# A decoder block on one core: bias copies issued one at a time, one conditional block in place of two, and 28 low parts on GpSimd

## The chip, the cores and the metric

The kernel runs on one core of a Trainium2 chip. The metric is the device time of one execution in microseconds (us). Engines are named as in the profile: PE (TensorE), PEld (its weight loads), DVE (VectorE), ACT (ScalarE), POOL (GpSimd) and SP (SyncE, which here only issues transfers).

## The reference

One layer of a decoder block on 512 tokens of width 1024, in float32. A wide input projection feeds two branches:

```
proj = jnp.einsum('bsd,de->bse', x, w_in[l])
(q_a, k_a, v_a, iq, ik, iw, q_r, k_r, v_r, g_r, gate_a, gate_r) = jnp.split(proj, offsets, axis=-1)
...
_, sel = lax.top_k(score, k_sel)                       # 128 keys of each query, by an indexer's score
bias = rel_bias[t5_bucket(posb[:, :, None] - pos_g)]   # by distance of positions, for 8 heads
logits = einsum(q, k_g) * dh**-0.5 + bias              # softmax over the chosen keys
...
h = sigmoid(gate_a) * (y_a @ w_attn_branch) + sigmoid(gate_r) * (y_r @ w_ret_branch)
x = layer_norm(ALPHA * x + h @ w_out);  x = layer_norm(ALPHA * x + relu(x @ w_up)**2 @ w_down)
```

`y_a` is the sparse attention, `y_r` a chunkwise retention (512 tokens in four chunks, rotated queries and keys). The positions given are 0 to 511, so each step from one token to the next is 1; the kernel must also be right for others.

## The kernel before

**Units.** All weights come in 140 units: units 0 to 7 are 128x324 (index projection), all others 128x1024, which is two blocks of 128 rows by 512 columns. Units 8 to 11 make `ka`, 12 to 15 `qa`, 16 to 19 `va`, 20 to 23 `qr`, 24 to 27 `kr`, 28 to 35 `vr`, 36 to 43 `gr`; then come the gates and branches, the output projection and the MLP. SP loads a unit (`load_unit`, tile `raw`, 4 buffers), ACT makes its high part (`split_hi`, `whi`, 3 buffers), DVE its low part `raw - whi` (`split_lo`, `wlo`, 3 buffers), and PE multiplies three times for each product (`mm3`): high by high, low by high, high by low. A unit of two blocks is thus 24 matmuls of 512 columns, for four banks (`group`). When the last unit of a group is done, an engine reads its four PSUM banks out (tag `m`, 4 buffers), so the first matmul of the next group waits until a bank has been read. For `qr` and `kr` that is DVE (`rope_evac`: one product into tile `rt` and two half products, L670 and L673), and POOL adds the two (`rnat`).

**What runs between.** At each step of a group a `tick` moves queued tasks on: the rotation tables, the index scores and their top 128 (`topk_task`: 16 rounds of MAX and MATCH_REPLACE on DVE for each of three query blocks; the mask `mk` of a block is the last of it), and the attention. An attention task needs a tile `bm`: a piece of the bias, loaded by SP from a DRAM tensor `bd` (`bm_task`), to which POOL adds the mask. So `bm` loads stand on SP's queue between the loads of units, and POOL's additions come in the order of its queue.

**The bias.** `bias_by_distance` makes one row `R8` of biases by distance for each head. For even positions eight transfers from ACT's queue (`bias_even`, 7.15 MB in all) lay that row out in DRAM as `bd`, once for each query. `uneven` is 0 when every step of the positions is 1. The function `bias` is called twice, behind the group of `ka` for heads 0 to 3 and behind that of `qa` for heads 4 to 7: each call loads `uneven` into a register of every engine and opens a conditional block, in which the four transfers stand. The second call has an other branch, `bias_general`, which makes the bias for any positions, with matmuls on PE; it is not run here. Its instructions stand in each engine's program all the same, and an engine skips them with an unconditional branch.

**What sets the order.** The program is recorded in the order of the code, and a scheduler then orders each engine's instructions inside a block by a simulated timeline; no instruction crosses the border of a conditional block. On the chip each engine runs its list in order.

Of the kernel before, what the change touches and what calls it, by code (L numbers as in the profile page):

```python
# [11 lines left out]
F32 = mybir.dt.float32  # L12
# [47 lines left out]
class Build:  # L60
# [67 lines left out]
    def split_hi(self, i):  # L128
        if i >= len(self.units) or i in self.whi:
            return  # L130
        hi = self.w.tile([P, *self.units[i][1:]], F32R, tag="whi", name=f"whi{i}", bufs=3)
        self.nc.scalar.copy(hi, self.raw[i])  # L132
        self.whi[i] = hi

    def split_lo(self, i):
# [3 lines left out]
        self.nc.vector.tensor_sub(lo, self.raw.pop(i), self.whi[i].bitcast(F32))  # L139
# [118 lines left out]
    def setup_small(self):  # L258
# [3 lines left out]
        self.posq = sm.tile([P, 4], I32, name="posq")  # L262
        nc.sync.dma_start(self.posq, d["posq"])
# [25 lines left out]
    def bias_tables(self):  # L289
# [9 lines left out]
        self.rbd = sm.tile([P, 3, 4, H], BF16, name="rbd")  # L299
        nc.vector.memset(self.rbd, 0.0)  # L300
        for q in range(4):
            r = slice(32 * q, 32 * q + 32)
            nc.vector.tensor_copy(self.rbd[r, :, q, :], parts[r])
# [36 lines left out]
    def bias_general(self):  # L340
        run, todo = [], [self.bias_prep()] + [self.bias_task(j, G) for j in range(NS) for G in range(8)]
        while run or todo:
            if todo:
                run.append(todo.pop(0))
            for g in list(run):
                if next(g, self) is self:
                    run.remove(g)

    def bias_by_distance(self):
# [5 lines left out]
        for i, sl in enumerate((slice(0, S), slice(S, W))):  # L355
# [4 lines left out]
            for p in range(3):  # L360
                nc.tensor.matmul(ps[:H, :n], lhsT=self.rbd[:, p, 0, :], rhs=oh[i][:, :n],
                                 start=p == 0, stop=p == 2)
# [3 lines left out]

    def bias_even(self, hs):

        for j in range(NS):
            w = self.pitch(j) + 1  # L370
            row = self.R8[hs, S - P * (j + 1):S - P * (j + 1) + w]
            src = bass.AP(tensor=row.tensor, offset=row.offset, ap=[[0, P], row.ap[0], row.ap[1]])
            self.nc.scalar.dma_start(self.bd[j][hs, :P * w].rearrange("h (q w) -> q h w", q=P), src)

    def bias_prep(self):

        nc = self.nc
        self.nd = []
        for j in range(NS):
            K = P * (j + 1)  # L380
            dn = self.alloc(dt=I32, name="dn")
            nc.gpsimd.tensor_tensor(dn[:, :K], self.posq[:, j:j + 1].to_broadcast([P, K]),
                                    self.posk[:, :K], op=OP.subtract)
            nv = self.allocs(2, name="nv")
            n, v = nv[0][:, :K], nv[1][:, :K]
            nc.vector.tensor_scalar(n, dn[:, :K], 0.0, NMAX, op0=OP.max, op1=OP.min)
            nc.vector.tensor_scalar(v, n, 1.0, None, op0=OP.max)
            nc.scalar.activation(v, v, AF.Ln, scale=0.0625)
            nc.vector.tensor_scalar(v, v, 16 / math.log(8), -0.49, op0=OP.mult, op1=OP.add)
            nc.vector.tensor_scalar(v, v, MAGIC, MAGIC - 1, op0=OP.add, op1=OP.max)  # L390
            nc.vector.tensor_scalar(v, v, MAGIC - 1, None, op0=OP.subtract)
            nb = self.alloc(dt=BF16, name="nb")
            nc.vector.scalar_tensor_tensor(nb[:, :K], n, 15.0, v, op0=OP.min, op1=OP.add)
            nd = self.dr.tile([P, K], BF16, name=f"nd{j}")
            nc.sync.dma_start(nd, nb[:, :K])
            self.free(dn, nb, nv)
            self.nd.append(nd)
            yield

    def bias_task(self, j, G):  # L400

        nc = self.nc
        K, C = P * (j + 1), P * j + 16 * (G + 1)
        while len(self.nd) <= j:
            yield
        yield from self.need(4)
        st = self.allocs(2, shape=(P, 2, K), dt=BF16, name="bst")
        for i in range(2):
            src = self.nd[j][16 * G:16 * G + 16, :].rearrange("(q g) k -> q g k", q=4)
            src = src[:, 2 * i:2 * i + 2].rearrange("q g k -> q (g k)")  # L410
            nc.sync.dma_start(st[i].rearrange("p g k -> p (g k)"),
                              src[:, None, :].to_broadcast([4, 32, 2 * K]))
        yield
        yield
        oh = self.allocs(2, shape=(P, 2, C), dt=BF16, name="boh")
        for i in range(2):
            nc.vector.tensor_scalar(oh[i], st[i][:, :, :C], self.bucket, None, op0=OP.is_equal)
        self.free(st)
        yield
        ps = self.ps.tile([P, S], F32, tag="s", name="bps", bufs=3)  # L420
        for p in range(3):
            for g in range(4):
# [720 lines left out]
```

## Time and profile before

| | |
|---|---|
| median of three runs | 893.34 us (891.0 to 894.33) |
| the profiled execution | 893.39 us, of which the profile's span is 891.6 us |
| PE busy | 852.8 us (96%) |
| DVE, ACT, POOL busy | 497.5 (56%), 300.2 (34%), 119.4 us (13%) |
| mean granted TensorE clock | 0.985 of full |

The profiled execution is as long as the median of the runs. PE is busy nearly all the time, so the time of the kernel is that of PE's matmuls and of the places where PE stands. "Busy" adds up instructions; the waits of an engine are listed by what released them. The granted clock is 1.00 at 2.4 GHz and 0.50 at 1.2 GHz.

### The profile page before, as it was taken

How to read it: one execution, taken by the hardware profiler on the slowest of the kernel's cores; microseconds unless marked ns; L12 is line 12 of the kernel's file. 1: busy time of each engine (PE TensorE's matmuls, PEld its weight loads, DVE VectorE, ACT ScalarE, POOL GpSimd, SP SyncE). 2: the span in 40 equal slices, each digit the busy share in tenths (PEclk: the TensorE clock that was granted, in tenths of full speed). 3: DMA queues.
4: the chain of work that ended last, by engine and by line, in shares of the span. 5: the costliest groups of instructions: out<-in, count | busy, mean ns of one | idle time of the engine just before them, and what ended most of it. 6: DMA issues, size and time to landing. Idle time of an engine off the chain costs nothing. (4 is left out here: it accounts for less than half of the span.)

```text
span 891.6 us, 11014 instructions
## 1 busy us (share of the span) xinstructions
PE 852.8 (96%) x4154; PEld 715.8 (80%) x4154; DVE 497.5 (56%) x973; ACT 300.2 (34%) x540; POOL 119.4 (13%) x135
## 2 busy tenths in 40 slices
PE   8996899799999999999999899999999999999996
PEld 7785788588877888888888689888888888888885
DVE  6787599943664466644256685344434433443447
ACT  4543426243454331313223313344114411441300
POOL 0000423411120021161022053000000000000002
PEclk9998899999999999999999999999999999999999
DMA  8876753233243021253433520233333333323302
GB/s 260 195 192 139 163 163 103 62 97 114 59 130 107 2 95 48 71 201 104 145 94 119 189 71 1 71 95 94 95 95 98 99 96 106 98 95 94 119 1 94
DMA packets 35994, 95.32 MB, mean 107 GB/s; under 512 B 4304, under 2 KB 12120, under 8 KB 35936
## 3 DMA queue, kind: packets, MB, share of 16 engines
q1 hardware_dynamic: 31712, 87.24, 31.4%
q10 hardware_dynamic: 4224, 7.32, 4.6%
q8 instruction: 34, 0.56, 0.3%
q14 instruction: 24, 0.20, 0.1%
HBM read 92.43 MB, written 9.44 MB: 114 GB/s over the span
## 5 line engine op out<-in xcount | busy, mean ns | idle before, releaser
L139 DVE TENSOR_TENSOR wlo<-raw,whi 128x1024 fp32r<-128x1024 f32 (+1 forms) x132 | 161.0, 1220 | 242.6 <-ACT whi L132 242.0
L132 ACT CAST whi<-raw 128x1024 fp32r<-128x1024 f32 (+1 forms) x132 | 134.0, 1016 | 332.7 <-PE mps L146 159.4
L147 PE MATMUL mps<-whi,xTl 128*128 128x512 f32 (+1 forms) x256 | 96.9, 388 | 10.9 <-issue 10.9
L145 PE MATMUL mps<-whi,xTh 128*128 128x512 f32 (+1 forms) x256 | 96.2, 394 | 6.7 <-DVE rt L673 5.7
L146 PE MATMUL mps<-wlo,xTh 128*128 128x512 f32 (+1 forms) x256 | 98.9, 389 | 0.0
L146 PE MATMUL mps<-x1Tl,whi 128*128 128x512 f32 x224 | 87.2, 389 | 0.0
L146 PE MATMUL mps<-wlo,hidh 128*128 128x512 f32 x224 | 87.2, 389 | 0.0
L145 PE MATMUL mps<-x1Th,whi 128*128 128x512 f32 x224 | 87.2, 389 | 0.0
L147 PE MATMUL mps<-whi,hidl 128*128 128x512 f32 x224 | 87.2, 389 | 0.0
L145 PE MATMUL mps<-whi,hidh 128*128 128x512 f32 x224 | 87.0, 389 | 0.0
L147 PE MATMUL mps<-x1Th,wlo 128*128 128x512 f32 x224 | 87.0, 389 | 0.0
L145 PE MATMUL mps<-xTh,whi 128*128 128x512 f32 x192 | 75.9, 396 | 1.5 <-ACT whi L132 1.5
L147 PE MATMUL mps<-xTh,wlo 128*128 128x512 f32 x192 | 74.5, 391 | 1.0 <-DVE wlo L139 1.0
L146 PE MATMUL mps<-xTl,whi 128*128 128x512 f32 x192 | 75.3, 392 | 0.0
L147 PEld LDWEIGHTS mps<-whi,xTl 128*128 128x128 f32 x256 | 48.6, 192 | 20.2 <-issue 11.3
L145 PEld LDWEIGHTS mps<-whi,xTh 128*128 128x128 f32 x256 | 48.5, 192 | 17.0 <-DVE rt L673 5.4
L146 PEld LDWEIGHTS mps<-wlo,xTh 128*128 128x128 f32 x256 | 49.2, 193 | 8.6
L254 POOL TENSOR_SCALAR rstd<-lnmv 128x1 f32<-128x1 f32 x8 | 5.1, 643 | 372.9 <-DVE lnmv L774 372.8
L146 PEld LDWEIGHTS mps<-wlo,hidh 128*128 128x128 f32 x224 | 42.1, 188 | 8.8
L147 PEld LDWEIGHTS mps<-x1Th,wlo 128*128 128x128 f32 x224 | 42.1, 188 | 8.7
L146 PEld LDWEIGHTS mps<-x1Tl,whi 128*128 128x128 f32 x224 | 42.1, 188 | 8.7
L147 PEld LDWEIGHTS mps<-whi,hidl 128*128 128x128 f32 x224 | 42.1, 188 | 8.7
(207 smaller groups left out, 1500.7 us busy)
## 6 DMA issues: line engine op xcount, KB each, us to landing
raw<-wp SPq DMA_DIRECT2D x136, 512.0 KB, 3.7
bd<-R ACTq DMA_DIRECT2D x2, 1278.0 KB, 28.1
xraw<-xT SPq DMA_DIRECT2D x8, 256.0 KB, 4.6
bm<-bd SPq DMA_DIRECT2D x8, 256.0 KB, 2.7
xn<-x SPq DMA_DIRECT2D x8, 256.0 KB, 4.5
out<-out SPq DMA_DIRECT2D x8, 256.0 KB, 2.0
bd<-R ACTq DMA_DIRECT2D x2, 1022.0 KB, 23.3
bm<-bd SPq DMA_DIRECT2D x8, 192.0 KB, 3.1
```

The source lines that it names most:

```text
L132: self.nc.scalar.copy(hi, self.raw[i])
L139: self.nc.vector.tensor_sub(lo, self.raw.pop(i), self.whi[i].bitcast(F32))
L145: mm(out, lhsT=a[0], rhs=b[0], start=first, stop=False)
L146: mm(out, lhsT=a[0], rhs=b[1], start=False, stop=False)
L147: mm(out, lhsT=a[1], rhs=b[0], start=False, stop=last)
L254: nc.gpsimd.tensor_scalar(t[:, :n], var, EPS, None, op0=OP.add)
```

## The change

Three things. First, `bias_even` becomes a task of its own: its eight transfers are always made, two for each query block (four heads each), with two steps between them, and each is issued behind the latest high part on ACT's queue (`issue_after(self.last_hi)`). Second, the two conditional blocks become one, behind the group of `va` (L835 and L836 of the changed kernel, where the task's flag is awaited first): it is entered only for uneven positions, and holds a new `bias_general` that uses no PE but over a thousand instructions of DVE. `preferred_fallthrough_block=False` lays the empty branch out first. Third, `split_lo` gives the low parts of units 16 to 43 to GpSimd. One small input transfer (`posq`) goes, and a tile `rbd` becomes smaller.

```diff
         hi = self.w.tile([P, *self.units[i][1:]], F32R, tag="whi", name=f"whi{i}", bufs=3)
-        self.nc.scalar.copy(hi, self.raw[i])
+        self.last_hi = self.nc.scalar.copy(hi, self.raw[i]).ins
...
-        self.nc.vector.tensor_sub(lo, self.raw.pop(i), self.whi[i].bitcast(F32))
+        engine = self.nc.gpsimd if 16 <= i < 44 else self.nc.vector
+        engine.tensor_sub(lo, self.raw.pop(i), self.whi[i].bitcast(F32))
...
-    def bias(self, hs):
-        tc = self.tc
-        uneven = self.nc.values_load(self.uneven[0:1, 0:1])
-        with tc.If(uneven == 0) as cmp:
-            self.bias_even(hs)
-        if hs.stop == H:
-            with cmp.Else():
-                self.bias_general()
-            self.flags.add("bias")
+    def bias_even(self):
+        yield from self.wait("R8")
+        for j in range(NS):
+            w = self.pitch(j) + 1
+            for h in range(0, H, 4):
+                row = self.R8[h:h + 4, S - P * (j + 1):S - P * (j + 1) + w]
+                src = bass.AP(tensor=row.tensor, offset=row.offset, ap=[[0, P], row.ap[0], row.ap[1]])
+                with self.tc.issue_after(self.last_hi):
+                    self.nc.scalar.dma_start(
+                        self.bd[j][h:h + 4, :P * w].rearrange("h (q w) -> q h w", q=P), src)
+                yield
+                yield
+        self.flags.add("even")
+
+    def bias_other(self):
+        uneven = self.nc.values_load(self.uneven[0:1, 0:1])
+        with self.tc.If(uneven, preferred_fallthrough_block=False):
+            self.bias_general()
+        self.flags.add("bias")
...
+            acc = self.allocs(H, name="acc")
+            for b in range(32):
+                if b:
+                    V.tensor_scalar(v, n, float(b), None, op0=OP.is_equal)
+                for h in range(H):
+                    w, a = rb[:, b * H + h:b * H + h + 1], acc[h][:, :K]
+                    if b == 0:
+                        V.tensor_scalar(a, n, 0.0, w, op0=OP.is_equal, op1=OP.mult)
+                    else:
+                        V.scalar_tensor_tensor(a, v, w, a, op0=OP.mult, op1=OP.add)
+            for h in range(H):
+                nc.sync.dma_start(self.bias_at(j, h, 1, 0, P, K).rearrange("q h k -> q (h k)"), acc[h][:, :K])
...
         self.queue([self.rope_prep()], delay=14)
+        self.queue([self.bias_even()], delay=12)
...
-        self.bias(slice(0, 4))
         self.qaT = self.allocs(4, name="qaT")
         yield from self.group(4, xT, tb, ev_copy(self.qaT, 0.125, "qa"), True)
-        self.bias(slice(4, 8))
-        self.free(self.posk)
...
         yield from self.group(4, xT, range(4), ev_va, False)
+        yield from self.wait("even")
+        self.bias_other()
+        self.free(self.posk)
```

**PE's list.** Before, PE comes to the second conditional block inside units 16 and 17. These rows stand ahead of the skipped part and at its start (`whi16` is the high part of unit 16, `bps` a bank of `bias_general`):

```order
L146 MATMUL mps_1781<-wlo16_837,xTh_117 128x512
L147 MATMUL mps_1781<-whi16_828,xTl_118 128x512
L332 TENSOR_LOAD uneven_185
L333 COMPARE_AND_BRANCH
L333 UNCONDITIONAL_BRANCH
L423 LDWEIGHTS rbd_173
L423 MATMUL bps_954<-boh_946,rbd_173 32x16
```

The skipped part has 768 rows. It ends like this, and the stream goes on inside unit 17:

```order
L423 LDWEIGHTS rbd_173
L423 MATMUL bps_1718<-boh_1714,rbd_173 32x512
L333 UNCONDITIONAL_BRANCH
L147 MATMUL mps_1763<-whi17_1750,xTl_120 128x512
L145 MATMUL mps_1763<-whi17_1750,xTh_121 128x512
```

In the changed kernel PE comes to the only conditional block inside units 20 and 21, and nothing of PE's stands in it:

```order
L149 MATMUL mps_2332<-whi20_991,xTl_118 128x512
L148 MATMUL mps_2321<-wlo21_2328,xTh_119 128x512
L149 MATMUL mps_2321<-whi21_2319,xTl_120 128x512
L147 MATMUL mps_2321<-whi21_2319,xTh_121 128x512
L344 TENSOR_LOAD uneven_180
L345 COMPARE_AND_BRANCH
L345 UNCONDITIONAL_BRANCH x2
L147 MATMUL mps_2344<-whi20_991,xTh_115 128x512
L148 MATMUL mps_2344<-wlo20_1001,xTh_115 128x512
L149 MATMUL mps_2344<-whi20_991,xTl_116 128x512
```

So the skip moved from unit 17 to unit 20 or 21, and on PE it went from 768 rows to none.

**DVE's list.** Before, DVE meets the second block right behind the first MAX of the second query block's top 128 (`sc2`; `mk1` is the mask of the block before it), and skips 88 rows there:

```order
L561 MATCH_REPLACE sc1_465<-m8_534,sc1_465 128x256
L139 TENSOR_TENSOR wlo18_1800<-raw18_839,whi18_1792 128x1024
L564 TENSOR_SCALAR mk1_224<-sc1_465 128x256
L560 MAX m8_785<-sc2_521 128x8
L332 TENSOR_LOAD uneven_185
L333 COMPARE_AND_BRANCH
L333 UNCONDITIONAL_BRANCH
L386 TENSOR_SCALAR nv_884<-dn_882 128x128
```

In the changed kernel it is behind the first MAX of the third query block (`sc3`), and the skipped part has 1,172 rows. These rows stand at its start:

```order
L530 MATCH_REPLACE sc2_516<-m8_772,sc2_516 128x384
L533 TENSOR_SCALAR mk2_220<-sc2_516 128x384
L529 MAX m8_954<-sc3_582 128x8
L344 TENSOR_LOAD uneven_180
L345 COMPARE_AND_BRANCH
L345 UNCONDITIONAL_BRANCH
L363 TENSOR_SCALAR nv_1045<-dn_1043 128x128
L364 TENSOR_SCALAR nv_1046<-nv_1045 128x128
```

And these at its end, where the third query block goes on (`qk` are the stacked parts of heads 0 and 1):

```order
L379 SCALAR_TENSOR_TENSOR acc_2003<-nv_1988,rbb_1041,acc_2003 128x512
L345 UNCONDITIONAL_BRANCH
L530 MATCH_REPLACE sc3_582<-m8_954,sc3_582 128x512
L565 TENSOR_TENSOR qk_2386<-qaT_674,qk_2386 64x512
L566 TENSOR_TENSOR qk_2388<-kaT_395,qk_2387 64x512
L567 TENSOR_TENSOR qk_2388<-kaT_395,qk_2387 64x512
L529 MAX m8_954<-sc3_582 128x8
L565 TENSOR_TENSOR qk_2395<-qaT_674,qk_2395 64x512
```

What moved: the block stands one query block later, between the masks `mk2` and `mk3`, its skipped part is 13 times as long, and the low parts of units 16 to 43 are gone from DVE's list. Behind the block, up to the third row of the rotation of `qr`'s first bank (L642), stand 10 MATCH_REPLACE, 9 MAX, six subtractions that make `qk`, four rows of softmax pieces for each of two heads, and three products.

**POOL's list.** Before, the additions of the masks stand alone with those of `rnat`:

```order
L580 TENSOR_TENSOR bm_1988<-bm_1988,mk1_224 128x256
L580 TENSOR_TENSOR bm_2024<-bm_2024,mk1_224 128x256
L580 TENSOR_TENSOR bm_2047<-bm_2047,mk2_225 128x384
L580 TENSOR_TENSOR bm_2076<-bm_2076,mk2_225 128x384
L580 TENSOR_TENSOR bm_2227<-bm_2227,mk0_223 128x128
L675 TENSOR_TENSOR rnat_2106<-rt_2101,rt_2102 128x512
L675 TENSOR_TENSOR rnat_2123<-rt_2118,rt_2119 128x512
L580 TENSOR_TENSOR bm_2284<-bm_2284,mk0_223 128x128
L675 TENSOR_TENSOR rnat_2148<-rt_2143,rt_2144 128x512
```

In the changed kernel the low parts of units 22 to 25 stand between the same additions (the loads of `bm` ahead of them come from SP's list, behind the conditional block, in which SP skips 33 rows, where before it skipped 100):

```order
L549 TENSOR_TENSOR bm_2339<-bm_2339,mk0_218 128x128
L549 TENSOR_TENSOR bm_2358<-bm_2358,mk0_218 128x128
L549 TENSOR_TENSOR bm_2381<-bm_2381,mk1_219 128x256
L549 TENSOR_TENSOR bm_2417<-bm_2417,mk1_219 128x256
L549 TENSOR_TENSOR bm_2440<-bm_2440,mk2_220 128x384
L549 TENSOR_TENSOR bm_2469<-bm_2469,mk2_220 128x384
L141 TENSOR_TENSOR wlo22_2371<-raw22_1003,whi22_2363 128x1024
L141 TENSOR_TENSOR wlo23_2430<-raw23_2330,whi23_2422 128x1024
L141 TENSOR_TENSOR wlo24_2501<-raw24_2373,whi24_2486 128x1024
L549 TENSOR_TENSOR bm_2620<-bm_2620,mk0_218 128x128
L141 TENSOR_TENSOR wlo25_2609<-raw25_2432,whi25_2600 128x1024
L644 TENSOR_TENSOR rnat_2499<-rt_2494,rt_2495 128x512
```

So each low part now waits for the additions that stand ahead of it, and an addition waits for its `bm` load and its mask.

## Rows read from the trace of the kernel before

**Rows 1.** Waits of PE: engine, line, releaser: total us, times, longest us.

```profile
PE mps L147 <- issue: 10.9, 1, 10.9
PE mps L145 <- DVE rt L673: 5.7, 2, 4.9
PE ptps L642 <- DVE pr L635: 4.4, 4, 1.7
```

**Rows 2.** Windows of PE: stretch, length, busy (instructions), granted clock, DMA share, GB/s.

```profile
80.00:90.00 10.00, 1.25 (x6) 0.67 1.02 187
90.00:100.00 10.00, 7.86 (x24) 0.64 1.01 192
...
170.00:180.00 10.00, 5.06 (x16) 0.83 0.00 0
```

**Rows 3.** Timeline of PE: start, us, instruction, [idle before, releaser].

```profile
73.83 0.39 PE L145 MATMUL mps<-whi,xTh 128*128 128x512 f32 x1
...
80.86 0.39 PE L147 MATMUL mps<-whi,xTl 128*128 128x512 f32 x1
92.14 0.79 PE L147 MATMUL mps<-whi,xTl 128*128 128x512 f32 x1 [10.89 <-issue]
...
97.53 0.39 PE L145 MATMUL mps<-whi,xTh 128*128 128x512 f32 x1
...
100.03 0.39 PE L147 MATMUL mps<-whi,xTl 128*128 128x512 f32 x1
```

**Rows 4.** DMA queues, 76 to 89 us: packets, MB, share of 16 engines.

```profile
q10 hardware_dynamic: 1170, 1.54, 80.6%
```

**Rows 5.** DMA queues, 89 to 92 us, same columns.

```profile
q8 instruction: 1, 0.02, 2.7%
```

**Rows 6.** Timeline of DVE.

```profile
76.06 0.29 DVE L564 TENSOR_SCALAR mk<-sc 128x256 bf16<-128x256 f32 x1
...
77.51 0.09 DVE L561 MATCH_VALUE_LOAD sc<-m,sc 128x8 f32 x1 [0.69 <-DVEq L333]
...
78.17 0.56 DVE L560 MAX8 m<-sc 128x8 f32<-128x384 f32 x1
...
79.42 0.56 DVE L560 MAX8 m<-sc 128x8 f32<-128x384 f32 x1
...
142.01 0.69 DVE L560 MAX8 m<-sc 128x8 f32<-128x512 f32 x1
...
143.53 0.69 DVE L560 MAX8 m<-sc 128x8 f32<-128x512 f32 x1
```

**Rows 7.** Waits of SP's queue, 70 to 101 us.

```profile
SPq L333 <- SPq L333: 17.1, 2, 16.6
```

**Rows 8.** DMA issues of the page: transfer, queue, count, KB each, median us to landing.

```profile
bd<-R ACTq DMA_DIRECT2D x2, 1278.0 KB, 28.1
...
bm<-bd SPq DMA_DIRECT2D x8, 64.0 KB, 2.6
```

**Rows 9.** Window of DVE, columns as in rows 2.

```profile
112.00:134.00 22.00, 21.66 (x51) 1.00 0.54 168
```

**Rows 10.** Groups by form, POOL, then DVE: busy us, mean ns, idle before.

```profile
L934 POOL TENSOR_TENSOR gt<-gt 128x512 f32<-128x512 f32 x8 | 12.5, 1585 | 61.2 <-DVE gt L930 61.2
...
L675 POOL TENSOR_TENSOR rnat<-rt 128x512 f32<-128x512 f32 x8 | 10.5, 1312 | 24.9 <-ACT whi L132 14.5 <-DVE rt L673 7.5 <-DVE rsum L634 2.7
...
L139 DVE TENSOR_TENSOR wlo<-raw,whi 128x1024 fp32r<-128x1024 f32 x124 | 157.1, 1267 | 239.3 <-ACT whi L132 238.7
...
L597 DVE TENSOR_TENSOR qk<-kaT,qk 64x512 fp32r<-64x512 f32 x8 | 6.0, 754 | 1.5 <-ACT qk L594 1.3
```

**Rows 11.** Timelines of POOL and DVE around 161 us.

```profile
161.13 1.29 POOL L675 TENSOR_TENSOR rnat<-rt 128x512 f32<-128x512 f32 x1 [0.18 <-DVE rt L673]
...
161.62 1.88 DVE L139 TENSOR_TENSOR wlo<-raw,whi 128x1024 fp32r<-128x1024 f32 x1
```

**Rows 12.** Waits of POOL.

```profile
POOL bm L580 <- DMA bm<-bd: 66.5, 14, 11.2
```

More of the change, by code (lines that the diff above doesn't have):

```diff
@@ L261, in setup_small @@
         nc.sync.dma_start(self.cst, d["cst"])
-        self.posq = sm.tile([P, 4], I32, name="posq")
-        nc.sync.dma_start(self.posq, d["posq"])
         self.posn = sm.tile([P, 4], I32, name="posn")
@@ L298, in bias_tables @@
                 nc.vector.tensor_sub(rb[:, i + 1], rb[:, i], parts[:, i])
-        self.rbd = sm.tile([P, 3, 4, H], BF16, name="rbd")
+        self.rbd = sm.tile([P, 3, H], BF16, name="rbd")
         nc.vector.memset(self.rbd, 0.0)
-        for q in range(4):
-            r = slice(32 * q, 32 * q + 32)
-            nc.vector.tensor_copy(self.rbd[r, :, q, :], parts[r])
+        nc.vector.tensor_copy(self.rbd[:32], parts[:32])
         step, odd = self.alloc(shape=(1, S), dt=I32, name="step"), self.alloc(shape=(1, S), name="odd")
@@ L326, in bias_at @@
                        ap=[[w, nq], [P * w + P, nh], [1, n]])
-    def bias(self, hs):
-        tc = self.tc
-        uneven = self.nc.values_load(self.uneven[0:1, 0:1])
-        with tc.If(uneven == 0) as cmp:
-            self.bias_even(hs)
-        if hs.stop == H:
-            with cmp.Else():
-                self.bias_general()
-            self.flags.add("bias")
-    def bias_general(self):
[L341 to L347, printed above, removed]
+    def bias_even(self):
[11 more added lines that the diff above has]
+        self.flags.add("even")
@@ new lines, in bias_other @@
+    def bias_other(self):
+        uneven = self.nc.values_load(self.uneven[0:1, 0:1])
+        with self.tc.If(uneven, preferred_fallthrough_block=False):
+            self.bias_general()
+        self.flags.add("bias")
+    def bias_general(self):
+        nc = self.nc
+        V = nc.vector
+        rb = self.alloc(name="rbb")
+        nc.sync.dma_start(rb[:, :32 * H], self.d["rbf"].to_broadcast([P, 32 * H]))
+        for j in range(NS):
+            K = P * (j + 1)
+            dn = self.alloc(dt=I32, name="dn")
+            nc.gpsimd.tensor_tensor(dn[:, :K], self.posn[:, j:j + 1].to_broadcast([P, K]),
+                                    self.posk[:, :K], op=OP.subtract)
+            nv = self.allocs(2, name="nv")
+            n, v = nv[0][:, :K], nv[1][:, :K]
+            V.tensor_scalar(n, dn[:, :K], 0.0, NMAX, op0=OP.max, op1=OP.min)
+            V.tensor_scalar(v, n, 1.0, None, op0=OP.max)
+            nc.scalar.activation(v, v, AF.Ln, scale=0.0625)
+            V.tensor_scalar(v, v, 16 / math.log(8), -0.49, op0=OP.mult, op1=OP.add)
+            V.tensor_scalar(v, v, MAGIC, MAGIC - 1, op0=OP.add, op1=OP.max)
+            V.tensor_scalar(v, v, MAGIC - 1, None, op0=OP.subtract)
+            V.scalar_tensor_tensor(n, n, 15.0, v, op0=OP.min, op1=OP.add)
+            acc = self.allocs(H, name="acc")
[10 more added lines that the diff above has]
+                nc.sync.dma_start(self.bias_at(j, h, 1, 0, P, K).rearrange("q h k -> q (h k)"), acc[h][:, :K])
+            self.free(dn, nv, acc)
+        self.free(rb)
@@ L365, in bias_by_distance @@
         self.free(bk, oh, ev)
[L367 to L422, printed above, removed]
-                nc.tensor.matmul(ps[32 * g:32 * g + 32, :C],
-                                 lhsT=self.rbd[:, p].rearrange("p q h -> p (q h)"),
-                                 rhs=oh[g // 2][:, g % 2, :], start=p == 0, stop=p == 2)
-        self.free(oh)
-        ev = self.alloc(name="bev")
-        nc.scalar.copy(ev[:, :C], ps[:, :C])
-        if C < K:
-            nc.gpsimd.memset(ev[:, C:K], 0.0)
-        yield
-        nc.sync.dma_start(self.bias_at(j, 0, H, 16 * G, 16, K), ev[:, :K])
-        self.free(ev)
@@ L436, in rope_prep @@
+        self.flags.add("R8")
     def rope_prep(self):
```

4 lines of the change are left out of this document (2 added, 2 removed).

## Prediction

> **What bounds the kernel now.** I read the list of what PE waited for first, because PE is busy 96% of the span: only what makes PE stand, or run at the lower clock, can change the time. The reader is to see that PE waits seldom, and that one wait is larger than all others together: 10.9 us in one piece, with no releaser that the profile shows ("issue"). Two waits for DVE's `rt` make 5.7 us, four for `pr` 4.4 us [rows 1]. The timeline of PE puts the large one at 81.3 to 92.1 us, inside units 16 and 17, exactly where its list has the second conditional block, behind which 768 rows are skipped [rows 3]. The windows show the second part of the price: the granted clock is 0.67 and 0.64 in the two stretches around the gap, so PE runs at 1.2 GHz for some time after it [rows 2].
>
> Why does a skip take 10.9 us? The queues' view shows it: in 76 to 89 us the bias copies (q10) hold 81% of the 16 DMA engines and PE's instruction queue (q8) moves nothing; its one packet comes in 89 to 92 us, and PE goes on at 92.1 [rows 3, 4, 5]. So PE waited for code behind a far branch, and the request stood some 8 us behind the copies. SP, which skips 100 rows, stood 16.6 us at the same line [rows 7]. DVE, which skips 88, lost 0.69 us [rows 6]. A short skip is nearly free, a far one is not. The Trainium skill says why ("Runtime: NRT & Kernel Launch", section "Instruction fetch mechanics"): a taken branch to code outside the two pages that an engine holds has to fetch by DMA; the trace agrees, with the packet just named.
>
> The second place is DVE. In 112 to 134 us it is busy 21.66 of 22 us [rows 9], with the top 128, the low parts and the rotation all on it. There the second wait arises: the `vr` group cannot start a bank because DVE is late in reading `kr`, 4.9 us [rows 1], and the clock falls to 0.83 in that stretch [rows 2].
>
> **The change part by part.** All sums are made against the profiled execution's 893.4 us, which is the median of the runs within 0.1 us.
>
> *The block on PE.* PE now skips no rows. Its own share of the block is a register load and branches over one row. The nearest row is DVE's block with a skip of 88 rows, 0.69 us [rows 6], and PE's matmuls in flight cover part of that; I take 0. So the gap of 10.9 us goes. The clock: from 92.14 to 97.53 stand 13 intervals of matmuls in 5.39 us; at full clock (11 intervals from 97.53 to 100.03, 0.227 us each) they take 2.95 [rows 3]. That is 2.4 us more. Sum: **-13.3 us**. Both ends: all of it, or none if PE's fetch stays.
>
> *The block on DVE.* Here the change adds a far skip: 1,172 rows. When does DVE come to it? `mk1` starts at 76.06; the low parts of units 16 to 18 stood ahead of it and go to POOL, 3 x 1.2 us, so 72.5. Then 16 rounds of the second query block at 1.25 us (from MAX to MAX) are 20.0, mask and first MAX of the third 1.0 [rows 6]: DVE branches near 94 us. The price of the skip lies between 0.69 us [rows 6] and 10.9 us [rows 1]. By length it is nearest to PE's skip, but 8 of those 10.9 us were the wait behind the copies. These are now issued one at a time from about 33 us on, the last at the start of unit 16, 73.8 us [rows 3]; a copy of the largest size landed after 28 us when four ran together [rows 8], so near 94 the last one is ending. I take 6 us, about half way: DVE goes on at 100.
>
> What is late next? Queued behind the branch on DVE, up to the release of `qr`'s first bank, are 19 steps of the third top 128 at 1.52 us a pair, 14.4 us [rows 6], six `qk` subtractions, 6 x 0.75 = 4.5 [rows 10], and some 3 us of short softmax rows and three products (an estimate: a MAX of 512 columns takes 0.69). So the bank is free at 100 + 21.9 = 121.9. PE begins unit 16 at 73.8; eight units of 24 matmuls at 0.227 us are 43.6, and the few attention matmuls about 1 us more: it wants the bank at 118.4. PE waits 3.5 us, plus about 1 us of lower clock (the 4.9 us wait near 170 left 16 matmuls in 5.06 us, where 3.6 would do [rows 2]: 1.4 lost). Sum: **+4.5 us**. With the ends of the price: 0 at 0.69; at 10.9 PE waits 8.4 and loses 2 more, +10.4.
>
> *The low parts on POOL, as DVE sees it.* 28 low parts of 1.27 us [rows 10] leave DVE, 12 of them between units 16 and 27. In the old kernel DVE was also idle for 13 us around 86 to 99, standing with PE; so ahead of `kr`'s rotation it gains 13 - 6 + 12 x 1.27 = 22 us while PE gains 13.3 - 4.5 = 9. It was 5 us late, so it is now early, and the two waits for `rt` go: 5.7 us, and the 1.4 us of clock. **-7.1 us**. Of the waits for `pr`, behind a relieved DVE, I give a third, **-1.5 us**; the rest lie in the last attention task, where nothing moves.
>
> *The same, as PE sees it.* A subtraction of 128x1024 on POOL is not in the trace. Nearest are two f32 inputs of 128x512: 1.31 us (`rnat`) and 1.59 (`gt`) [rows 10]; doubled, 2.6 to 3.2. I take 2.6. With three `whi` buffers a high part is made two units ahead of its use, 10.9 us, so after 1.1 us of ACT and 2.6 of POOL there are 7 us of slack for what stands ahead on POOL: mask additions that wait for `bm` loads (66.5 us over 14 waits, at most 11.2 [rows 12]). Each such load stands behind a unit's load on SP, and that one waits for the low part four units back; so a turn is 2.6 us to landing [rows 8], about 1 us of issue, 1 to 2 additions of at most 1.4, and 2.6: 7.5 us at worst, with 2.6 where no `bm` stands between. On average over the list 5.5 us for a unit, against 6 to 7 of PE with the attention in between. **0 us**; the cover is the two units of lead. If it is gone, each microsecond too many costs 28.
>
> *Copies always made, spaced.* The same eight transfers. They held 81% and more of the engines in one burst; spread over some 60 us they share with unit loads, which have 4 buffers of lead. **0 us**, as in the old kernel, where neither burst let PE wait for a `raw`.
>
> Sum: 893.4 - 13.3 + 4.5 - 7.1 - 1.5 = **876.0 us**. Behind unit 43 the lists are alike, so nothing is given back later.
>
> **The rivals.**
>
> *DVE's skip pays in full* (the copies are still running at 94): +10.4 in place of +4.5, **882**. For it: the same mechanism and a longer skip. Against: only the last copy can still run.
>
> *DVE's skip is hidden*: it comes to 3 us or less, PE waits nothing for `qr`, and more of the small waits go: **870**. For it: a code packet itself is a small transfer, and PE went on within 3 us of it.
>
> *SP's skip stays slow.* Before, SP stood 16.6 us [rows 7]. If its 33 rows cost as much, the first `bm` loads land near 94.5 + 16.6 + 3.5 = 114.6, six additions and the low part of unit 22 behind them end at 121, and PE wanted it at 106.5: +14.5 and 2 of clock, so **892**, no change. Against it: DVE's 88 rows cost 0.69.
>
> *POOL is too slow: slower than before.* The place is units 22 to 43, where POOL has the low parts besides its additions. DVE and POOL hinder each other: a low part on DVE took 1.88 us beside a `rnat` that began 0.5 us earlier, against 1.27 [rows 10, 11]. If such waits go both ways, a low part on POOL grows. At 4.8 us a turn comes to 7.7 on average, 0.8 over PE's, and 22 units eat the 17.4 us of gain: from there on the kernel is slower. At 5.5 it is 1.5 x 22 = 33 lost, **909**. Against: most of what DVE does there reads PSUM or one tile. The Trainium skill speaks for this rival ("SBUF — State Buffer", section "Who interferes with whom"): a VectorE instruction with two SBUF inputs contends with a GpSimd instruction that reads SBUF, and the later one waits for all of the other. By that rule, taken at its worst, each of the 24 `qk` subtractions would also wait 2.6 us.
>
> **How the numbers follow.** Forecast 48% (its own range 871 to 881), full skip 18%, hidden skip 14%, slow SP 10%, slow POOL 10%. The range takes the first three and the way to the fourth: 867 to 888. Half a per cent, 4.5 us, is about what a measurement of this kernel tells from no change. Faster by more: 0.80 (the first three); within: 0.11; slower: 0.09.
>
> **What would show it.** Right: no idle of 10 us on PE near 81, granted clock 1.00 from 80 to 100; a gap on DVE at its branch of 3 to 9 us, with an instruction packet at its end; PE waiting up to 8 us for `rt` near 118, none near 170; low parts on POOL at 2.4 to 3.2 us, and no PE wait for `wlo`. Wrong: waits of PE for POOL's `wlo`, additions on POOL waiting over 7 us with a low part behind them, a gap on SP at its branch, or a PE gap at the new block.

## The result, and the profile after

The changed kernel takes **872.0 us** (median of 4 runs, 871.1 to 874.3) against 893.2 us for the kernel before on the same chip: ratio 0.977, 95% interval 0.974 to 0.980, so 2.3% faster. The profiled execution took 872.2 us with a span of 870.4 us. The forecast was 876.0 with a range of 867 to 888.

The profile's page says where the 21.2 us of span came from: PE's busy time is 848.1 us in place of 852.8, so 4.7 us are matmuls at a higher clock, and 16.5 us are time in which PE no longer stands. First, what PE waits for now (engine, line, releaser: total us, times, longest us):

```profile
PE mps L147 <- DVE xn L953: 4.0, 1, 4.0
PE mps L147 <- ACT inat L803: 3.7, 1, 3.7
PE ptps L611 <- DVE pr L604: 2.6, 4, 1.2
PE mps L147 <- DVE rt L642: 1.2, 2, 1.0
PE mps L148 <- POOL wlo L141: 1.1, 1, 1.1
```

The wait of 10.9 us in one piece [rows 1] is gone, the two for `rt` went from 5.7 to 1.2 us, those for `pr` from 4.4 to 2.6. New is the second row, near the start, for `inat`. The windows of PE (stretch, length, busy with instructions, granted clock, DMA share, GB/s) show the same by place:

```profile
20.00:30.00 10.00, 6.83 (x23) 0.83 0.81 302
80.00:90.00 10.00, 10.00 (x46) 1.00 0.97 310
90.00:100.00 10.00, 10.00 (x46) 1.00 0.41 128
170.00:180.00 10.00, 10.00 (x50) 1.00 0.27 75
```

Where 6 and 24 matmuls stood at a clock of 0.67 and 0.64 [rows 2], there are now 46 and 46 at full clock. The first row is the new loss: ACT's list now has the high part of unit 9 ahead of all four copies of `inat`; it waits for that unit's load while four full banks wait for ACT. On ACT's timeline:

```profile
21.74 1.04 ACT L132 CAST whi<-raw 128x1024 fp32r<-128x1024 f32 x1 [3.84 <-DMA raw<-wp]
22.69 1.41 ACT L803 COPY inat<-mps 128x324 f32<-128x324 f32 x4
```

DVE meets its branch at 96.9 us, behind the first MAX of the third query block, and its timeline goes on 3.34 us later; these rows, and the one of PE at the bank that was to be late, are the test of the term of +4.5 us:

```profile
96.22 0.69 DVE L529 MAX8 m<-sc 128x8 f32<-128x512 f32 x1
100.25 0.09 DVE L530 MATCH_VALUE_LOAD sc<-m,sc 128x8 f32 x1 [3.34 <-issue]
...
121.51 0.41 DVE L642 TENSOR_TENSOR rt<-mps,cs 128x256 f32<-128x256 f32 x1
```

```profile
75.15 0.39 PE L147 MATMUL mps<-whi,xTh 128*128 128x512 f32 x1
...
122.07 0.47 PE L147 MATMUL mps<-whi,xTh 128*128 128x512 f32 x1 [0.18 <-DVE rt L642]
```

The bank came free at 121.9 us and PE wanted it at 121.9: it waited 0.18 us. Groups by form, of POOL and DVE (busy us, mean ns of one, idle before):

```profile
L141 POOL TENSOR_TENSOR wlo<-raw,whi 128x1024 fp32r<-128x1024 f32 x28 | 67.5, 2415 | 75.0 <-ACT whi L132 71.9 <-issue 3.1
...
L566 DVE TENSOR_TENSOR qk<-kaT,qk 64x512 fp32r<-64x512 f32 x8 | 8.0, 1006 | 0.2
```

A low part takes 2.4 us on POOL, and ahead of the 28 POOL stood 72 us for high parts, 37 of them ahead of the first alone: between the first and the last it had some 35 us of room. One of DVE's three kinds of subtraction for `qk`, the one shown, grew from 0.75 us [rows 10] to 1.0. SP's wait at the block, 16.6 us before [rows 7], is 1.7 now, and the largest copies land after 18.9 us, not 28.1 [rows 8]:

```profile
SPq L345 <- SPq L345: 2.1, 2, 1.7
```

```profile
bd<-R ACTq DMA_DIRECT2D x2, 1278.0 KB, 18.9
```

Last, landmarks: the first matmul of the retention's state (tile `kvps`) by the view of one tile, in the kernel before and then in the changed one (shortest, median and longest ns, first and last start):

```profile
L724 PE MATMUL kvps<-vr,rnat x48: 270/275/276, 302.9 to 362.4; 128*128 128x128 f32 x48
```

```profile
L693 PE MATMUL kvps<-vr,rnat x48: 270/275/275, 281.9 to 341.3; 128*128 128x128 f32 x48
```

Of the 21.2 us, 21.0 are won before 282 us; nothing is given back behind it.

### The profile page after: what moved, and what is told of

Read it like the earlier page. It is cut to its first block, busy times and chain, and to the rows that moved or that the text cites. A ratio compares the mean times of both kernels' runs of the same rounds, so it can differ in the third digit from the quotient of the medians.

```text
span 870.4 us, 10972 instructions
## 1 busy us (share of the span) xinstructions
PE 848.1 (97%) x4154; PEld 713.6 (82%) x4154; DVE 476.7 (55%) x942; ACT 300.6 (35%) x540; POOL 184.8 (21%) x163
## 5 line engine op out<-in xcount | busy, mean ns | idle before, releaser
L141 DVE TENSOR_TENSOR wlo<-raw,whi 128x1024 fp32r<-128x1024 f32 (+1 forms) x104 | 125.0, 1202 | 223.5 <-ACT whi L132 220.0
L141 POOL TENSOR_TENSOR wlo<-raw,whi 128x1024 fp32r<-128x1024 f32 x28 | 67.5, 2415 | 75.0 <-ACT whi L132 71.9
## 6 DMA issues: line engine op xcount, KB each, us to landing
bd<-R ACTq DMA_DIRECT2D x2, 1278.0 KB, 18.9
```

Of the source, the lines that this page charges most:

```text
L141: engine.tensor_sub(lo, self.raw.pop(i), self.whi[i].bitcast(F32))
```

## The experiments

All ratios are against the kernel before, run in the same series.

**The two parts alone.** The kernel before with the low parts on POOL and nothing else changed:

```diff
-        self.nc.vector.tensor_sub(lo, self.raw.pop(i), self.whi[i].bitcast(F32))
+        engine = self.nc.gpsimd if 16 <= i < 44 else self.nc.vector
+        engine.tensor_sub(lo, self.raw.pop(i), self.whi[i].bitcast(F32))
```

> The kernel before with one edit: the low parts of units 16 to 43 on GpSimd. My theory (two separate gains: PE's far skip, and DVE's relief): the gap of 10.9 us near 81 us and its slow clock stay, the two waits for rt near 160 and 170 us (5.7 us and 1.4 of clock) go: 885 us, 883 to 888. Rival (the conditional block is the whole gain, DVE was late only because it stood with PE): 893. Rival (all of the gain is the relief): 873.

Measured: 883.5 us, ratio 0.990 (0.987 to 0.992), as the theory said. PE's gap stays, the waits for `rt` shrink to 1.3 us:

```profile
PE mps L147 <- issue: 11.7, 1, 11.7
...
PE mps L146 <- DVE rt L674: 1.3, 2, 1.1
```

The changed kernel with all low parts left on DVE:

```diff
-        engine = self.nc.gpsimd if 16 <= i < 44 else self.nc.vector
-        engine.tensor_sub(lo, self.raw.pop(i), self.whi[i].bitcast(F32))
+        self.nc.vector.tensor_sub(lo, self.raw.pop(i), self.whi[i].bitcast(F32))
```

> The changed kernel with all low parts back on DVE. My theory: the gap of 10.9 us and 2.4 of clock are gone, but DVE carries 12 more low parts (15 us) up to the rotation of kr and PE comes there 13 us earlier, so PE's waits for rt are larger than the 5.7 us of before, 8 to 12 us: 883 us, 879 to 887. Rival (the GpSimd part is worth nothing): 872. In this kernel one low part (unit 23) stands behind DVE's skip of 1,172 rows, so a skip of over 8 us would show as a PE wait for wlo.

Measured: 882.6 us, ratio 0.988 (0.986 to 0.990). No gap; the waits for `rt` are larger than before, 7.3 us in all (8 to 12 were expected; the time agrees also because this kernel waits 5.2 us for `inat` near the start, which the theory did not have), and one of them, 2.97 us at 126.6 us, is at the bank of `qr` of which the prediction spoke:

```profile
126.58 0.47 PE L146 MATMUL mps<-whi,xTh 128*128 128x512 f32 x1 [2.97 <-DVE rt L641]
...
171.13 0.58 PE L146 MATMUL mps<-whi,xTh 128*128 128x512 f32 x1 [4.37 <-DVE rt L641]
```

So about 10 us come from each part, and the product of the two ratios, 0.978, lies inside the interval of the whole.

**The block taken out.** The changed kernel without its conditional block (it then makes no bias for other positions):

```diff
-        uneven = self.nc.values_load(self.uneven[0:1, 0:1])
-        with self.tc.If(uneven, preferred_fallthrough_block=False):
-            self.bias_general()
```

> The changed kernel without the conditional block (for positions in steps of 1 alone; the part for other positions is left out). My theory (DVE's skip of 3.3 us is hidden, PE and the others pay nothing for the block): 872, within 1.5 us of the changed kernel. Rival (the block still costs every engine a register load and a branch, and DVE's 3.3 us reach PE through the rotation of qr): 867 to 869.

Measured: 869.1 us, ratio 0.973 (0.971 to 0.975). What the remaining block costs is at most some 3 us; the interval overlaps that of the changed kernel, so it is not told from nothing. The kernel before without its blocks, copies made plainly in their place (so again no bias for other positions):

```diff
-        tc = self.tc
-        uneven = self.nc.values_load(self.uneven[0:1, 0:1])
-        with tc.If(uneven == 0) as cmp:
-            self.bias_even(hs)
+        self.bias_even(hs)
         if hs.stop == H:
-            with cmp.Else():
-                self.bias_general()
             self.flags.add("bias")
```

> The kernel before without its two conditional blocks: the eight copies stand plainly at the same two places in the code, in bursts of four (for positions in steps of 1 alone; the part for other positions is left out). My theory (PE stood for code behind a far branch): no gap near 81 us, 13.3 us less; DVE no longer stands with PE, so its waits for rt may grow by some us: 880 to 884. Rival (the burst of copies makes PE stand, whatever the branch): the gap stays, 890 or more.

Measured: 891.7 us, ratio 0.999 (0.997 to 1.001): a miss. The gap near 81 us is gone, but another of 13 us has come. Without the borders of the blocks the scheduler puts all eight copies together from 30.9 us on, and ACT stands while it issues them; its evacuations are late and PE stands. Timeline of ACT, then of PE:

```profile
37.66 15.50 ACTq L368 DMA_DIRECT2D bd<-R  x2
53.21 0.58 ACT L484 CAST iqT<-iqps 64x512 fp32r<-64x512 f32 x1 [15.69 <-issue]
```

```profile
58.91 0.80 PE L530 MATMUL scps<-ikTh,iqT 128*128 128x256 f32 x2 [13.06 <-ACT ikTh L240]
```

A second attempt to take away only what is skipped: both blocks and their copies kept, the other branch left out (so here too no bias for other positions).

```diff
         if hs.stop == H:
-            with cmp.Else():
-                self.bias_general()
             self.flags.add("bias")
```

> The kernel before with its two conditional blocks and their copies kept at their places, but the other branch left out: no engine has rows to skip (the bias of other positions is not made). Theory (the gap of 10.9 us is the far skip): PE's gap near 81 us goes with its stretch of half clock, no other wait takes its place because the copies still go out in two bursts of four, and DVE is as loaded as before: 878 to 882 us. Rival (the second burst at this place makes PE stand whatever it skips): a gap of 8 us or more stays near 81 us, 888 to 893 us. Second rival (DVE, no longer stopped beside PE, is later at rt by as much): waits for rt grow beyond 10 us, 886 us.

Measured: 904.3 us, ratio 1.014 (1.011 to 1.017), a larger miss by the same mechanism: nothing held the second block at its place any more, it went right behind the first, and eight copies in one burst kept ACT for 29 us where four take it 5.3 us in the kernel before:

```profile
31.13 29.37 ACTq L371 DMA_DIRECT2D bd<-R  x8
```

```profile
64.31 1.09 PE L518 MATMUL ikps<-ident,ik 128*128 128x128 f32 x4 [24.32 <-DVE ik L513]
```

**The copies not spaced.** The changed kernel, its eight copies issued one behind the other:

```diff
-                with self.tc.issue_after(self.last_hi):
-                    self.nc.scalar.dma_start(
-                        self.bd[j][h:h + 4, :P * w].rearrange("h (q w) -> q h w", q=P), src)
-                yield
-                yield
+                self.nc.scalar.dma_start(
+                    self.bd[j][h:h + 4, :P * w].rearrange("h (q w) -> q h w", q=P), src)
```

> The changed kernel with its eight copies issued one right behind the other on ACT's queue (no issue_after, no steps between). Theory from the run in which both blocks were taken out of the kernel before: ACT stands at its own queue for about 13 us while the first copies drain, its evacuations and high parts come late, PE stands 10 to 14 us between 35 and 60 us and runs 13.65 us at half clock behind it: 883 to 890 us. Rival (what the prediction said, spacing the copies is worth 0 us): 870 to 874 us, with no wait of PE beyond those of the changed kernel.

Measured: 891.1 us (881.2 to 893.5 over 12 runs), ratio 0.998 (0.996 to 1.001), just above the expected range. The profiled run is the shortest of them (one other took 882.9, the other ten 889.4 and more), so what the ten lose beyond it is not shown. It has PE waiting at the same place; ACT's issues take up to 6.3 us each:

```profile
50.94 6.32 ACTq L335 DMA_DIRECT2D bd<-R  x1
57.29 1.05 ACT L132 CAST whi<-raw 128x1024 fp32r<-128x1024 f32 x1 [5.80 <-issue]
```

```profile
52.27 0.58 PE L501 MATMUL scps<-ikTh,iqT 128*128 128x256 f32 x1 [6.13 <-DVE iqT L456]
61.56 0.39 PE L501 MATMUL scps<-ikTh,iqT 128*128 128x256 f32 x1 [3.23 <-ACT rl L506]
```

The spacing is worth 19 us by the medians: nearly as much as the whole change brings.

**PE's far skip at a quiet place.** The changed kernel, in whose single block the former `bias_general` stands, with 768 rows of PE and 88 of DVE (`rbd` and the input `posq` come back with it):

```diff
     def bias_general(self):
+        run, todo = [], [self.bias_prep()] + [self.bias_task(j, G) for j in range(NS) for G in range(8)]
...
-            acc = self.allocs(H, name="acc")
-            for b in range(32):
...
+                nc.tensor.matmul(ps[32 * g:32 * g + 32, :C],
+                                 lhsT=self.rbd[:, p].rearrange("p q h -> p (q h)"),
+                                 rhs=oh[g // 2][:, g % 2, :], start=p == 0, stop=p == 2)
```

> The changed kernel with the former bias_general, which has 768 rows on PE, in the body of its single conditional block at units 20 and 21, where the bias copies have ended (its small input posq and the wider rbd come back). Theory (8 of the 10.9 us were the code's wait behind the copies): PE's gap at the block is 2.5 to 4 us, with one instruction packet in it, little or no half clock behind it: 873 to 878 us. Rival (a skip of this length costs 10.9 us by itself): gap 9 to 12 us and 13.65 us at half clock, 883 to 888 us.

Measured: 872.3 us, ratio 0.978 (0.976 to 0.981), 0.7 us under the expected range. PE's timeline has a gap of 4.0 us at the block, and the queues in 97 to 102 us show the one packet of PE's instructions in it, with no copy beside it (packets, MB, share of 16 engines):

```profile
101.55 0.47 PE L147 MATMUL mps<-whi,xTh 128*128 128x512 f32 x1 [4.02 <-ACT qk L599]
```

```profile
q1 hardware_dynamic: 572, 0.40, 33.1%
q8 instruction: 1, 0.02, 1.6%
```

The view names ACT's `qk` as releaser, of which this matmul reads nothing; the packet is the likelier one. So the same skip costs 4.0 us here and 10.9 in the burst [rows 1]. Behind it PE runs 3.4 us at half clock. That the kernel is no slower than the changed one has a reason at its start: it has no wait for `inat` (there is none among PE's waits) and begins unit 16 at 71.98 us, 3.2 us earlier. By the count of PE's matmuls it is 2.7 us behind the changed kernel after the block, and level with it again by 165 us.

**The burst put back.** Four copies more, into a scratch tensor that nobody reads, just ahead of the block: once in the changed kernel, once in the one with PE's far skip.

```diff
+        for j in range(NS):
...
+            with self.tc.issue_after(self.last_hi):
+                self.nc.scalar.dma_start(
+                    self.bx[j][:, :P * w].rearrange("h (q w) -> q h w", q=P), src)
         uneven = self.nc.values_load(self.uneven[0:1, 0:1])
```

> The changed kernel with four copies more, of heads 4 to 7 into a scratch tensor that nobody reads, issued on ACT's queue just ahead of the conditional block, so that DVE's far skip falls into a burst like the one that PE's fell into before. Theory (what made the skip dear was the burst): DVE stands 8 to 11 us at its branch in place of 3.3, the bank of qr is free 5 to 7 us later and PE waits as much for rt, with some half clock: 877 to 881 us. Rival (a far skip costs 3.3 us on DVE with copies or without): DVE's gap 3 to 4 us, 871 to 875 us.

Measured: 887.0 us, ratio 0.993 (0.991 to 0.996). DVE stands 8.82 us at its branch, as the theory said, but the time is 6 us above it, since ACT and SP stand still longer and PE waits for ACT's evacuation of `va`, 15.7 us, and not for `rt`. Timeline of DVE; waits of all engines in 90 to 125 us:

```profile
98.33 0.69 DVE L537 MAX8 m<-sc 128x8 f32<-128x512 f32 x1
107.83 0.09 DVE L538 MATCH_VALUE_LOAD sc<-m,sc 128x8 f32 x1 [8.82 <-issue]
```

```profile
POOL qrT L855 <- SPq L353: 20.5, 1, 20.5
ACT L570 <- SPq L353: 18.6, 1, 18.6
...
PE mps L147 <- ACT va L839: 15.7, 1, 15.7
```

Why SP? The instruction lists say it: SP's branch over the block carries waits on all eight DMA semaphores, and ACT's first row behind the block waits for one of them. In the kernel before SP's branch at the second block has four such waits.

```
SP   L353 UNCONDITIONAL_BRANCH [waits DMAHW0_49,DMAHW1_49,DMAHW2_49,DMAHW3_49,DMAHW4_49,DMAHW5_49,DMAHW6_49,DMAHW7_49]
ACT  L570 ACT_TABLE_LOAD [waits DMAHW1_49]
```

A DMA semaphore is a counter that a transfer raises when it lands. In this run SP goes on at 116.9 us, when the last of the four copies lands. In the kernel before it went on at 94.1, when its own last unit load landed, issued at 76.2 beside the copies; two of the bias copies landed only at 100.5 and 104.4. So SP stands there for the transfers in flight whose semaphores its branch waits for, however few rows it skips.

> The run with the former bias_general in the block (768 rows on PE, whose gap there was 4.0 us) with the same four copies more, into a scratch tensor, just ahead of the block. Theory: PE's gap grows from 4.0 to 9 to 11 us and 13.65 us of half clock follow, as in the kernel before: 881 to 886 us. Rival (the difference between 10.9 us before and 4.0 us lay in the place or the length of the code, not in the copies): gap 4 to 5 us, 872 to 875 us.

Measured: 885.3 us, ratio 0.991 (0.988 to 0.994). PE's gap at its skip grows from 4.0 to 6.8 us, less than expected, and PE then waits 6.1 us for ACT, which stood as in the run above:

```profile
105.00 0.77 PE L147 MATMUL mps<-whi,xTh 128*128 128x512 f32 x1 [6.78 <-issue]
117.81 0.80 PE L147 MATMUL mps<-whi,xTh 128*128 128x512 f32 x1 [6.06 <-ACT va L876]
```

The time is inside the expected range, the gap is not: the added copies lengthen it by 3 us, not by the 7 that lie between 4.0 and 10.9. Half clock came in two stretches of 6.8 us, where the kernel before had one of 13.65, 8.7 of them inside its gap. The packet of PE's code (q8) that falls into each gap says where the difference lies (times in us; the last column counts the packets of copies, q10, that start in the gap, so it grows with the gap too):

| run | gap from | packet starts | PE goes on | copies' packets |
|---|---|---|---|---|
| low parts on POOL alone | 76.96 | 85.53 | 88.67 | 1135 |
| kernel before | 81.25 | 89.28 | 92.14 | 944 |
| far skip with four copies | 98.22 | 102.11 | 105.00 | 560 |
| far skip at a quiet place | 97.53 | 98.59 | 101.55 | 0 |

In all four PE goes on 2.9 to 3.1 us after its packet starts. What differs is the wait for the packet: 8.6, 8.0, 3.9 and 1.1 us. DVE's far skip shows the same on the other instruction queue (q14): in the changed kernel the gap starts at 96.91 us, its first packet at 98.43; with the four copies ahead of the block 99.01 and 105.98; in both DVE goes on 1.8 to 1.9 us after that start. So what a far skip costs beyond its price at a quiet place is the wait for its packet, and adding the copies alone brings that wait about. Why it is 3.9 us here and 8.0 before is open; the last copy was issued 10 us ahead of the gap here, and 2 us ahead of it before.

**POOL's reserve.** Each of the 28 low parts made twice:

```diff
-        engine.tensor_sub(lo, self.raw.pop(i), self.whi[i].bitcast(F32))
+        raw = self.raw.pop(i)
+        engine.tensor_sub(lo, raw, self.whi[i].bitcast(F32))
+        if 16 <= i < 44:
+            engine.tensor_sub(lo, raw, self.whi[i].bitcast(F32))
```

> The changed kernel with each of the 28 low parts on POOL made twice in a row (4.8 us in place of 2.4; the second writes the same values again). By the prediction's reckoning of POOL's turn (break-even at 4.8 us for a low part): PE waits for wlo by some 18 us and the gain is gone, 888 to 896 us. Rival (POOL stood 72 us waiting for high parts in the changed kernel, and 28 x 2.4 = 68 us more find their place there, so that the loads of bm are hardly ever what it waits for): PE's waits for wlo stay under 6 us, 872 to 878 us.

Measured: 904.9 us, ratio 1.015 (1.012 to 1.017), above both. No wait for `wlo` stands in PE's list of waits; PE waits 12.8 us in one piece for DVE's `qk`. DVE's timeline shows a subtraction of 64x512 that lasts 17.66 us, and POOL's a stream without a gap beside it:

```profile
102.20 0.69 DVE L568 TENSOR_TENSOR qk<-qaT,qk 64x512 fp32r<-64x512 f32 x1
...
105.22 17.66 DVE L568 TENSOR_TENSOR qk<-qaT,qk 64x512 fp32r<-64x512 f32 x1
```

```profile
104.22 2.52 POOL L552 TENSOR_TENSOR bm<-bm,mk 128x128 f32<-128x128 f32 x4
...
117.70 4.64 POOL L144 TENSOR_TENSOR wlo<-raw,whi 128x1024 fp32r<-128x1024 f32 x2
133.42 2.34 POOL L142 TENSOR_TENSOR wlo<-raw,whi 128x1024 fp32r<-128x1024 f32 x1 [11.08 <-ACT whi L132]
```

DVE got through at 122.88 us, half a microsecond after POOL's last instruction ended (122.34). Neither expectation had this; POOL's throughput was not what decided. A stream without a gap is not enough to bring it about (the next run has one that let three such subtractions through), and why it came here is open.

**The start mended.** The high part of unit 9 held behind the last copy of `inat`, beside the changed kernel in the same series:

```diff
+        if i == 9:
+            with self.tc.issue_after(self.last_inat):
+                self.last_hi = self.nc.scalar.copy(hi, self.raw[i]).ins
+        else:
             self.last_hi = self.nc.scalar.copy(hi, self.raw[i]).ins
```

> The changed kernel with one order set by hand: on ACT the high part of unit 9 comes behind the last of the four copies of inat (the scheduler had put it ahead of all four, where it waits for the load of its unit while four full PSUM banks wait for ACT). Theory: PE's wait of 3.7 us near 23 us and the 3.4 us of half clock behind it go, 3 to 4 us less than the changed kernel: 867.5 to 870 us. Rival (PE then waits as long for the high part of unit 9, or the loss comes back later): 871 to 874 us.

> The changed kernel as it is, run beside the three others of this call so that they can be set against it: 871 to 874 us.

Measured: 869.2 us (867.6 to 869.5), ratio 0.973 (0.970 to 0.975); the changed kernel beside it 871.8 us (868.5 to 873.3), ratio 0.975 (0.973 to 0.978). The start is as expected: 8.96 us busy at full clock in 20 to 30 us, against 6.83 at 0.83, and unit 16 begins at 71.15 us, 4.0 earlier than in the changed kernel. But the whole of it is lost again near 100 us, where DVE's `qk` subtractions meet POOL's additions and low parts. POOL's timeline, DVE's and PE's, and the window of PE:

```profile
96.10 5.22 POOL L553 TENSOR_TENSOR bm<-bm,mk 128x128 f32<-128x128 f32 x6
```

```profile
98.62 1.93 DVE L571 TENSOR_TENSOR qk<-kaT,qk 64x512 fp32r<-64x512 f32 x1
...
101.30 2.90 DVE L569 TENSOR_TENSOR qk<-qaT,qk 64x512 fp32r<-64x512 f32 x1
```

```profile
100.60 0.58 PE L591 MATMUL qkps<-qk 128*128 128x256 f32 x1 [2.95 <-DVE qk L571]
```

```profile
95.00:105.00 10.00, 5.54 (x16) 0.66 0.35 112
```

The changed kernel has 46 matmuls in that window. At the landmark `kvps` nothing of the gain is left: 282.2 us here, 281.9 in the changed kernel's first profile (283.1 in the one of this series). The 2.8 us by which the span is shorter than in that first profile come near 485 us, where PE waits 2.2 us for `xn` and not 4.0, and no half clock follows:

```profile
L697 PE MATMUL kvps<-vr,rnat x48: 270/275/275, 282.2 to 341.7; 128*128 128x128 f32 x48
```

```profile
PE mps L151 <- DVE xn L957: 2.2, 1, 2.2
```

So, by these profiles, the time is in the range of the theory by luck: what happened is the rival's second half, the loss came back later. Of the kernels that leave nothing out it is the fastest, 2.6 us under the changed one by the medians; the two intervals overlap, so the step between them is not shown beyond doubt.

## Why the prediction was right, and where it was not

**The block on PE, -13.3 us: right.** The gap and its half clock are gone. The reading that the far skip was dear because of the copies, 8 of its 10.9 us, holds: the packet was waited for 8.0 us, and 1.1 at a quiet place. The Trainium skill ("Runtime: NRT & Kernel Launch", section "Instruction fetch mechanics") says that a taken branch out of the pages that an engine holds forces a fetch by DMA; the 16 KB packet inside the gap of 4.0 us agrees. But two sentences beside it were wrong. The wait of 10.9 us is the largest, but not larger than all others together, which make 19.8. And SP's 16.6 us [rows 7] were put down to a skip of 100 rows. They are the waits on DMA semaphores that its branch carries, above all the one for its own unit load: under copies SP stood 18.6 us for 33 rows, without them 1.7. "A short skip is nearly free, a far one is not" needs the addition that a border also collects transfers in flight. It also explains why the rival "SP's skip stays slow" did not come: the copies' last packet ended at 91.6 us, and SP came to its branch at 96.3.

**The block on DVE, +4.5 us: the mis-sized term.** It came to 0.2 us. The skip cost 3.3 us, not 6, but DVE reached it 3 us later than reckoned, so it went on at 100.25 us where 100 was forecast, and the bank came free at 121.9, as forecast: luck, two errors that cancel. What failed is the other side: "it wants the bank at 118.4". PE began unit 16 at 75.15, not 73.8 (the loss at the start), and from there to 121.9 are 46.7 us, of which 43.6 are the eight units: the attention matmuls between them (14 of them) took 3 us, not 1. PE's side is thus close to the rival "DVE's skip is hidden" (870 us), though the skip was not under 3 us. DVE was exactly in time, with no reserve: in the run with the block alone, where DVE also had its low parts, the wait at this bank was 2.97 us. In the run with the burst put back the gap on DVE was 8.82 us, near the dear end of the price; what it costs PE by itself is not shown, since PE waited for ACT there.

**DVE's relief, -7.1 and -1.5 us: right.** The waits for `rt` fell by 4.5 us and the lower clock of 160 to 180 us (0.91 before, 1.00 now) is gone; the waits for `pr` fell by 1.8. The prediction put the wait of 4.9 us into the stretch of 112 to 134 us; it lies at 170.8 to 175.7, which changes no term. The part alone brought 9.9 us by its medians, where the prediction had 8.6 for it.

**POOL, 0 us: right in size, incomplete in reason.** 2.4 us for a low part against the forecast 2.6, and one wait for `wlo` of 1.1 us. But the break-even at 4.8 us was reckoned by POOL's turn, and the doubled run did worse, 12.6 us over the kernel before, with DVE held up beside POOL. The rule that the prediction quoted beside that rival ("SBUF — State Buffer", section "Who interferes with whom", of the Trainium skill) is the mechanism that fits and that had to be priced: by it a VectorE subtraction of two SBUF inputs and a GpSimd instruction that reads SBUF exclude each other, one waiting for the whole of the other. It was taken at one POOL instruction for each `qk` subtraction; the trace of the doubled run has one subtraction waiting through a stream of POOL instructions, 17.66 us.

**Copies spaced, 0 us: right only beside the old bursts.** The term compared them with two bursts of four, each held at its place by a block. Where the blocks went and the copies were not spaced, they fell together: PE waited 13 us for it in the kernel before without blocks, and the changed kernel lost 19 us by the medians. So the spacing carries the first term. The prediction named unit loads as what a burst could delay, and not ACT, which issues the copies and stands while it does so.

**Not in the sum: the start.** The wait for `inat` is 3.7 us with a clock of 0.83 in 20 to 30 us; the kernel before lost some 3.1 us in smaller waits (1.5, 1.0 and 0.6), at full clock. By unit 16 the changed kernel is 1.3 us behind. The loss comes from the order of ACT's list near unit 9, but the change does touch the start, with its smallest part: leaving aside the run where the order was set by hand, all seven profiles without the transfer of `posq` and with the smaller `rbd` have this wait (3.7 to 5.2 us), and none of the six with both of the old pieces has it. Which of the two pieces turns the order, and how, was not tried.

Together: -13.3 + 0.2 for the block, -5.9 and -1.8 for DVE's waits, +1.1 for `wlo`, and +1.3 at the start are -18.4 us; the span fell by 21.2. The 2.8 us between are not assigned. So the forecast of 876.0 was 4 us high mostly for the term of DVE's block; two losses that it did not have and the unassigned gain nearly cancel.

## What to carry to other kernels

A conditional block is a border: code behind it may have to be fetched, and the engine that loads data may wait there for transfers in flight, so put it where no large transfer is running, whatever is skipped. Taking a border away also frees the scheduler to bunch what the border had kept apart; large copies need an order of their own, and the engine that issues them stands while they queue. When work moves from VectorE to GpSimd, look not only at GpSimd's room but at which VectorE instructions read two SBUF tiles beside a long stream on GpSimd.

## What the runs showed of the hardware that was not expected

- ACT stands while it issues large copies when several are under way: four of 0.5 to 1.28 MB (3.6 MB) took it 5.3 us, eight (7.2 MB) 29.4 us; spaced in the changed kernel, each took 0.5 to 0.6 us.
- One VectorE subtraction of 64x512, 0.69 us when alone, lasted 17.66 us beside a stream on GpSimd without a gap; beside the shorter streams of the changed kernel the three subtractions of this shape had means of 0.9 to 1.0 us, and the longest took 2.8. In the run with the start mended, six additions on GpSimd without a gap (5.2 us) let three of them through in 1.0 to 1.9 us each.
- A skip of 768 rows on PE took 4.0 us in a quiet stretch and 6.8 to 11.7 beside copies, one of 1,172 rows on DVE 3.3 and 8.8 us. PE went on 2.9 to 3.1 us after its packet of code started, DVE 1.8 to 1.9 us after; the rest was waiting for the packet.
